# Weight loads on two DMA queues, and stores of gates and gated activations issued from ScalarE, in a hybrid decoder layer

## The chip, the cores and the metric

The kernel runs on one core of a Trainium2 chip. The metric is the device time of one execution in microseconds; the time before the change is the median of three runs. Engines are named as in the profile: PE is TensorE (PEld its weight loads), DVE is VectorE, ACT is ScalarE, POOL is GpSimd and SP is SyncE. "SPq" and "ACTq" stand for the instructions by which SP and ACT issue DMAs.

## What is computed

One decoder layer (DEPTH is 1) on 256 tokens of width 2048, all in float32:

```python
h = rmsnorm(x, g_mix)
proj = h @ w_in                        # 2048 x (3*2048 + 3*2048): q, k, v of 16 heads, three gates
gates = sigmoid(proj[..., 3 * MIX_WIDTH:])
o_a = stick_breaking_attention(...)    # 4 heads
o_b = moba_attention(...)              # 6 heads; here one causal block of 256 keys
o_c = dilated_attention(...)           # 6 heads, windows with dilations 1, 4, 16
merged = (gates[:, :, 0] * (flat(o_a) @ w_branch[:ea])
          + gates[:, :, 1] * (flat(o_b) @ w_branch[ea:eb])
          + gates[:, :, 2] * (flat(o_c) @ w_branch[eb:]))
x = x + merged @ w_out
h2 = rmsnorm(x, g_ffn)
gu = h2 @ w_gu                         # 2048 x 11264
x = x + (silu(gu[..., :D_FF]) * gu[..., D_FF:]) @ w_down    # 5632 x 2048
```

## The kernel before

**Products in two parts.** Each float32 operand is kept as a high part, rounded to float32r, and a low part, the difference. `product` (L162) makes one product of a 128x128 activation tile with a 128x512 weight tile from three matmuls (L164 high times high, L165 high times the weights' low part, L166 low times high). Weights come from HBM as tiles of 128 partitions x 2 x 512 (512 KB, two rows of tiles). `split` (L109) makes the parts: ACT casts to `w_hi`, DVE subtracts and writes `w_lo`. There are 5 buffers each for `w_hi` and `w_lo`.

**Column pairs.** q and k of the four groups of heads, the gates (but for two chunks) and all of w_gu are made two column chunks at a time by `project_pair` (L325). Of the 2048 rows, the chunks 0 and 1 (`WC`, 1024 rows) are multiplied by a scheme of seven products in place of eight, whose weights are partly sums of weight tiles; the other 1024 rows are multiplied plainly, by `rest` (L340). So a pair has two kinds of weight tiles:

- *Weights that sums are made of*, `g_raw`: four quarters, b11, b12, b21 and b22, of two tiles each, loaded by `quarter` (L312) through `load` (L282) into 6 buffers. DVE adds them into `u` (L321: b11 + b12) and changes them in place (`add_into`, L308 and L310). `begin_pair` (L315) loads b11, b12 and b21 of the next pair near the end of the current one (L376); b22 is loaded at L353.
- *Plain weights*, `w_raw`: eight tiles in a pair (four for each of the two column chunks), loaded by `rest` through `load` into 4 buffers, each read by one cast and one subtraction.

The results of a pair go to the PSUM accumulators X, Y (`ps` or `qs`) and Z, V (`z` and `v`, or, in the qk units, the other one of `ps` and `qs`). The seven products come as forms: 1 into X, 2 into Y, 5 into Z, then two plain tiles into V and Z (L354, L355), form 6, a plain tile, form 7, a plain tile, form 3, two plain tiles, form 4, two plain tiles. ACT copies X and Z to SBUF in between (`snapshot`, L303), since both are written again.

**The queues.** All weights are issued by SP, one after the other in the program's order: `fetch` (L105) pins each load to that order, and a load whose buffer isn't free holds all that follow. POOL issues the rest: the bias tables of a group's softmax (L657, two buffers, free when DVE has added the table, L588), the stores of the gates to the DRAM tile `gate_mem` (`keep_gate`, L673) and their loads (L777), x and x1 (L402, L810, L929), the stores of gated activations to `a_mem` (L865 and L879) and their loads `a_raw` (L900). ACT issues the DMA transposes of the gated activations (L852): a chunk made in pair c goes out during pair c + 1 (`turn_out`), comes back in pair c + 2, where ACT joins its halves (`turn_in`, L857) and, from chunk 3 on, it is stored to `a_mem`.

**Stages in time.** v, q, k and attention (to about 310 us), gates (310 to 555), w_branch (530 to 620), w_out (620 to 710), w_gu in 11 pairs (710 to 1170), w_down (from 1170 on; its loads don't go through `fetch`). The order of all instructions that aren't pinned is set by a scheduler when the program is built; it sees the changed queues and may place attention's steps elsewhere among the matmuls.

Of the kernel before, what the change touches and what calls it, by code (L numbers as in the profile page):

```python
# [18 lines left out]
P = 128  # L19
# [10 lines left out]
NB = 512  # L30
# [27 lines left out]
def hybrid_block(ctx: ExitStack, tc: tile.TileContext, x, w_in, w_branch, w_out, w_gu, w_down, rel_bias, xT, gains,  # L58
                 onehot, extra, out):
    nc = tc.nc  # L60
    x, out = x[0], out[0]
    w_in, w_branch, w_out, w_gu, w_down = (w[0] for w in (w_in, w_branch, w_out, w_gu, w_down))
# [36 lines left out]
    def banks():  # L99

        turn.reverse()
        return [acc.tile([P, NB], F32, name=turn[1]) for _ in range(2)]


    def fetch(dst, src):  # L105

        tc.keep_in_program_order(nc.sync.dma_start(dst, src))

    def split(hi, lo, src, pin=False):  # L109
        for op in nc.scalar.copy(hi, src), nc.vector.tensor_sub(lo, src, hi.bitcast(F32)):  # L110
            if pin:
                tc.keep_in_program_order(op)
# [169 lines left out]
    def load(w, k, col0, pl=None):  # L282

        raw = pl.tile([P, 2, NB], F32, name="g_raw", bufs=6 if pl is gx else 4) if pl else wpool.tile([P, 2, NB], F32, name="w_raw", bufs=4)
        (nc.sync.dma_start if w is w_down else fetch)(raw, w[k * P:(k + 2) * P, col0:col0 + NB].rearrange("(k p) n -> p k n", p=P))
        return raw

    def parts(src):
# [14 lines left out]
    def snapshot(ps):  # L303
        sb = half_kb()
        nc.scalar.copy(sb, ps)
        return sb
# [5 lines left out]
    def quarter(acts, w, kh, col0):  # L312
        return [load(w, 4 * c + 2 * kh, col0, gx) for c in acts.wc]

    def begin_pair(acts, w, colA, colB):  # L315

        b11, b12 = (quarter(acts, w, 0, col0) for col0 in (colA, colB))
        p11 = [parts(b) for b in b11]
        u = [gx.tile([P, 2, NB], F32, name="u") for _ in acts.wc]
        for a, b, d in zip(b11, b12, u):  # L320
            nc.vector.tensor_add(d, a, b)  # L321
        b21 = quarter(acts, w, 1, colA)
        return p11, b12, u, b21, [parts(b) for b in b21]

    def project_pair(acts, w, colA, colB, begun=None, nxt=None):  # L325

        cols = (colA, colB)
        X, Y = banks()  # L330
        Z, V = others()

        def form(ps, f, srcs, start, stop, split=False):
            for i, c in enumerate(acts.wc):
                wh, wl = srcs[i] if split else parts(srcs[i])
                for j in range(2):
                    product(ps, *acts.form(f, c, j), wh[:, j], wl[:, j], start and i + j == 0,
                            stop and i + j == len(acts.wc))

        def rest(n, k, p0, p1, start=False, stop=False):  # L340
            wh, wl = parts(load(w, k, cols[n]))
            for t, ps in ((1, p1), (0, p0)):
                for j in range(2):
                    product(ps, *acts.plain(t, k + j), wh[:, j], wl[:, j], bool(start and t == 1 and j == 0), stop and j == 1)

        ks = [k for c in range(KT // 4) if c not in acts.wc for k in (4 * c, 4 * c + 2)]
        p11, b12, u, b21, p21 = begun or begin_pair(acts, w, colA, colB)
        form(X, 1, p11, True, True, True)
        s1 = snapshot(X)
        form(Y, 2, p21, True, False, True)  # L350
        form(Z, 5, u, True, True)
        z5 = snapshot(Z)
        b22 = quarter(acts, w, 1, colB)  # L353
        rest(1, ks[0], Z, V, start=True)  # L354
        rest(1, ks[1], Z, V)  # L355
        add_into(u, b22)
        form(X, 6, u, False, True)
        x2 = snapshot(X)
        rest(1, ks[2], Z, V)
        add_into(b12, b22)  # L360
        form(X, 7, b12, False, True)
        x3 = snapshot(X)
        rest(1, ks[3], Z, V, stop=True)
        nc.vector.tensor_sub(z5, z5, x3)
        c22 = half_kb()
        nc.vector.tensor_add(c22, V, z5)
        form(Z, 3, b22, False, True)
        c12 = half_kb()
        nc.vector.tensor_sub(c12, Z, x2)
        for k in ks[:2]:  # L370
            rest(0, k, Y, X)
        add_into(u, b21)
        form(X, 4, u, False, False)
        for k in ks[2:]:
            rest(0, k, Y, X, stop=k == ks[-1])
        ahead = begin_pair(*nxt) if nxt else None  # L376
        c11 = half_kb()
        nc.vector.tensor_add(c11, Y, s1)
        return (c11, X, c12, c22), ahead
# [287 lines left out]
    gate_mem = dram.tile([3, 4, NT, P, NB], F32, name="gate_mem")  # L667

    def keep_gate(c, b, srcs):
        for t in range(NT):  # L670
            gt = half_kb()
            nc.scalar.activation(gt, srcs[t], AF.Sigmoid, scale=rstd[:, t:t + 1])
            nc.gpsimd.dma_start(gate_mem[b, c, t], gt)  # L673

    heads = {}

# [38 lines left out]
    def pair_of(kind, what):  # L715
        if kind == "qk":
            return hs, w_in, what * NB, NH * HD + what * NB
        if kind == "gates":
            return hs, w_in, gate_col(*what[0]), gate_col(*what[1])
# [13 lines left out]
    for (kind, what), after in zip(units, units[1:] + [(None, None)]):  # L733
        if kind == "gates" and what[0] == chunks[4]:
            finish_stages(slow_stages)
            pat.close()
            acc2 = ctx.enter_context(tc.tile_pool(name="acc2", bufs=1, space=PSUM))
            others = beside
            o = Columns(pool(ph1, "o", "left"), "o", NH)
            for i in range(NH // 4):  # L740
                at_split[split_count[0] + 22 * i + 12] = [lambda k=4 * i: split_o(k)]
        nxt = pair_of(*after)
        if kind in ("qk", "gates"):
            ps, ahead = project_pair(*pair_of(kind, what), ahead, nxt)
            if others is in_turn:
                turn.reverse()
        else:
            ps = project(h, 0, w_in, 0, KT, V0 + what * NB if kind == "v" else gate_col(*what),
                         *((ps0, FIRST) if (kind, what) == ("v", 0) else ()))
            ahead = begin_pair(*nxt) if nxt else None  # L750
        finish_stages(stages)
        if kind == "v":
            keep_v(what, ps)
        elif kind == "qk":
            keep_qk(what, *ps)
        elif kind == "gate":
            keep_gate(*what, ps)
        else:
            keep_gate(*what[0], ps[:2])
            keep_gate(*what[1], ps[2:])  # L760
# [11 lines left out]
    for c in range(4):  # L772
        ms = [half_kb() for _ in range(NT)]
        for b, (k0, nk) in enumerate(((0, H_A), (H_A, H_B), (H_A + H_B, H_C))):
            gt = [half_kb() for _ in range(NT)]
# [39 lines left out]
    for c in range(4):  # L815
        xc = load_x(c, nc.gpsimd.dma_start)
        ps = project(m, 0, w_out, 0, KT, c * NB)
        if c == 3:
            ahead = begin_pair(h2, w_gu, 0, D_FF)
        keep_x1(c, ps, xc)  # L820
    pm.close()
# [20 lines left out]
    a_mem = dram.tile([NF // 4, P, 4, S], F32, name="a_mem")  # L842
# [14 lines left out]
    def turn_in(c, t, keep):  # L857

        st = turning.tile([P, NB], F32, name="joined").rearrange("p (k q) -> p k q", k=4)
        tc.keep_in_program_order(nc.scalar.copy(st.bitcast(U16).rearrange("p k (q b) -> p b k q", b=2),  # L860
                                                keep[t].rearrange("p (b k) q -> p b k q", b=2)))
        if c < EARLY:
            at_split.setdefault(split_count[0] + IN_PARTS[t], []).append(lambda: a.put(c, t, st, True))
        else:
            nc.gpsimd.dma_start(a_mem[c, :, :, t * P:(t + 1) * P], st)  # L865

    def to_a_by_dma(c, srcs):

# [5 lines left out]
    def to_a(c, srcs):  # L874
        for t in range(NT):
            pt = transpose4(srcs[t])
            st = half_kb().rearrange("p (k q) -> p k q", k=4)
            nc.scalar.copy(st, pt)
            nc.gpsimd.dma_start(a_mem[c, :, :, t * P:(t + 1) * P], st)  # L879
            yield  # L880

    for c in ORDER[:EARLY]:
        a.place(pe, c)
    for c in range(D_FF // NB):
        nxt = (h2, w_gu, (c + 1) * NB, D_FF + (c + 1) * NB) if c + 1 < D_FF // NB else None
        (g0, g1_, u0, u1), ahead = project_pair(h2, w_gu, c * NB, D_FF + c * NB, ahead, nxt)
        sg = [half_kb() for _ in range(NT)]
        for t, (g, u) in enumerate(((g0, u0), (g1_, u1))):
            nc.scalar.activation(sg[t], g, AF.Silu, scale=rstd2[:, t:t + 1])
            nc.vector.scalar_tensor_tensor(sg[t], u, rstd2[:, t:t + 1], sg[t], op0=ALU.mult, op1=ALU.mult)  # L890
        if c < NF // 4 - 2:
            to_a_by_dma(c, sg)
        else:
            stages.append(to_a(c, sg))
# [153 lines left out]
```

## Time and profile before

| | |
|---|---|
| Median of 3 runs | 1428.85 us (1427.88 to 1429.82) |
| Profiled execution | 1427.54 us, span 1425.8 us |
| TensorE clock granted | 1.00 |
| HBM read | 293.17 MB |
| SP's queue (q1) | 277.38 MB, 58.0% of the 16 DMA engines' time |
| POOL's queue (q0) | 29.45 MB, 5.9% |
| ACT's queue (q10) | 5.80 MB, 2.8% |

How to read it: a busy time is the union of an engine's instructions. Matmuls are pipelined, so a busy PE may still lose time between the starts of its matmuls; its weight loads (PEld) don't overlap each other and show such gaps. An idle time names what ended it (`<-`). In the table of DMA issues the last number is the median time from issue to landing; in the view of a tile the three numbers of a group are the shortest, median and longest duration in ns. In the view of waits the numbers are microseconds in total, times, and the longest.

### The profile page before, as it was taken

What the parts mean: (1) busy time and instruction counts of PE and PEld (TensorE: products, weight loads), DVE (VectorE), ACT (ScalarE), POOL (GpSimd) and SP (SyncE); (2) the same over time, 40 slices, a digit from 0 to 9 for tenths busy, and PEclk for the clock granted to TensorE, in tenths of its full rate; (3) what the DMA queues carried; (4) which work ended last, traced back from release to release, by engine and by line L of the source; (5) the groups of instructions that cost most, each with busy time, mean ns of one, the idle gap of its engine ahead of it and who ended that gap; (6) DMA issues with size and microseconds to landing.
All of it is one profiled execution on the core that took longest, in us unless ns stands there. A gap on an engine that the chain in (4) does not pass through costs nothing. (4 is left out here: it accounts for less than half of the span.)

```text
span 1425.8 us, 17593 instructions
## 1 busy us (share of the span) xinstructions
PE 1411.4 (99%) x6297; PEld 1159.1 (81%) x6297; DVE 1190.0 (83%) x1265; ACT 909.5 (64%) x1160; POOL 65.1 (5%) x121
## 2 busy tenths in 40 slices
PE   8999999999999999999999999999999999999998
PEld 6888788888888888888888887778888888788887
DVE  7898797867799997876689999999999998886775
ACT  7767777767666665444456677676777776654453
POOL 1000000000000002100100000000000010100000
PEclk9999999999999999999999999999999999999999
DMA  9764547374656757866686667577977786776552
GB/s 331 277 221 135 205 134 247 108 250 162 222 177 236 256 195 276 297 224 213 220 299 221 216 190 233 187 219 244 268 223 218 250 237 228 251 238 235 191 172 94
DMA packets 174056, 313.76 MB, mean 220 GB/s; under 512 B 29800, under 2 KB 32384, under 8 KB 173968
## 3 DMA queue, kind: packets, MB, share of 16 engines
q1 hardware_dynamic: 144672, 277.38, 58.0%
q0 software_dynamic: 8992, 29.45, 5.9%
q10 hardware_dynamic: 20304, 5.80, 2.8%
q8 instruction: 49, 0.80, 0.2%
q14 instruction: 39, 0.32, 0.1%
HBM read 293.17 MB, written 14.70 MB: 216 GB/s over the span
## 5 line engine op out<-in xcount | busy, mean ns | idle before, releaser
L110 DVE TENSOR_TENSOR w_lo<-w_raw,w_hi 128x1024 fp32r<-128x1024 f32 x332 | 403.3, 1221 | 122.4 <-ACT w_hi L110 119.4
L110 ACT CAST w_hi<-w_raw 128x1024 fp32r<-128x1024 f32 x332 | 346.3, 1050 | 171.4 <-PE qs L166 53.4
L110 ACT CAST w_hi<-g_raw 128x1024 fp32r<-128x1024 f32 x184 | 190.8, 1052 | 111.2 <-PE ps L166 31.9
L110 ACT CAST w_hi<-u 128x1024 fp32r<-128x1024 f32 x138 | 145.0, 1053 | 155.5 <-DVE u L310 77.5
L110 DVE TENSOR_TENSOR w_lo<-g_raw,w_hi 128x1024 fp32r<-128x1024 f32 x184 | 219.1, 1220 | 30.0 <-ACT w_hi L110 29.0
L110 DVE TENSOR_TENSOR w_lo<-u,w_hi 128x1024 fp32r<-128x1024 f32 x138 | 164.3, 1220 | 21.4 <-ACT w_hi L110 20.8
L165 PE MATMUL ps<-w_lo,h_hi 128*128 128x512 f32 x352 | 137.9, 392 | 1.2 <-DVE w_lo L110 1.2
L166 PE MATMUL ps<-w_hi,h_lo 128*128 128x512 f32 x352 | 137.3, 390 | 0.0
L164 PE MATMUL ps<-w_hi,h_hi 128*128 128x512 f32 x352 | 131.9, 391 | 0.0
L165 PE MATMUL qs<-w_lo,h_hi 128*128 128x512 f32 x332 | 129.7, 391 | 0.0
L166 PE MATMUL qs<-w_hi,h_lo 128*128 128x512 f32 x332 | 129.2, 390 | 0.0
L164 PE MATMUL qs<-w_hi,h_hi 128*128 128x512 f32 x332 | 122.9, 391 | 0.0
L310 DVE TENSOR_TENSOR u<-u,g_raw 128x1024 f32<-128x1024 f32 x80 | 94.1, 1218 | 0.0
L165 PEld LDWEIGHTS ps<-w_lo,h_hi 128*128 128x128 f32 x352 | 66.1, 188 | 15.5 <-DVE w_lo L110 1.9
L166 PEld LDWEIGHTS ps<-w_hi,h_lo 128*128 128x128 f32 x352 | 66.1, 188 | 13.6
L164 PEld LDWEIGHTS ps<-w_hi,h_hi 128*128 128x128 f32 x352 | 65.9, 188 | 13.3
L166 PEld LDWEIGHTS qs<-w_hi,h_lo 128*128 128x128 f32 x332 | 62.3, 188 | 12.8
L165 PEld LDWEIGHTS qs<-w_lo,h_hi 128*128 128x128 f32 x332 | 62.3, 188 | 12.8
L164 PEld LDWEIGHTS qs<-w_hi,h_hi 128*128 128x128 f32 x332 | 62.3, 188 | 12.7
L321 DVE TENSOR_TENSOR u<-g_raw 128x1024 f32<-128x1024 f32 x40 | 48.7, 1219 | 20.9 <-DMA g_raw<-in_w_in 16.3
L165 PE MATMUL v<-w_lo,h_hi 128*128 128x512 f32 x120 | 48.0, 400 | 2.9 <-DVE w_lo L110 2.7
L310 DVE TENSOR_TENSOR g_raw<-g_raw 128x1024 f32<-128x1024 f32 x40 | 47.1, 1219 | 0.0
(386 smaller groups left out, 2940.8 us busy)
## 6 DMA issues: line engine op xcount, KB each, us to landing
w_raw<-in_w_in SPq DMA_DIRECT2D x116, 512.0 KB, 5.0
g_raw<-in_w_gu SPq DMA_DIRECT2D x88, 512.0 KB, 5.7
w_raw<-in_w_gu SPq DMA_DIRECT2D x88, 512.0 KB, 6.3
g_raw<-in_w_in SPq DMA_DIRECT2D x72, 512.0 KB, 5.4
w_raw<-in_w_down SPq DMA_DIRECT2D x64, 512.0 KB, 4.7
w_raw<-in_w_branch SPq DMA_DIRECT2D x32, 512.0 KB, 5.9
w_raw<-in_w_out SPq DMA_DIRECT2D x32, 512.0 KB, 4.7
g_raw<-in_w_down SPq DMA_DIRECT2D x24, 512.0 KB, 5.3
```

The lines of the kernel that those rows point to most:

```text
L110: for op in nc.scalar.copy(hi, src), nc.vector.tensor_sub(lo, src, hi.bitcast(F32)):
L164: nc.tensor.matmul(ps, ah, wh, start=start, stop=False, **how)
L165: nc.tensor.matmul(ps, ah, wl, start=False, stop=False, **how)
L166: nc.tensor.matmul(ps, al, wh, start=False, stop=stop, **how)
L310: tc.keep_in_program_order(nc.vector.tensor_add(d, d, a))
L321: nc.vector.tensor_add(d, a, b)
```

## The change

A second way to load is added, on POOL's queue, also pinned to the program's order. `load` uses it for `g_raw` tiles where the one-element list `own_queue` says so; plain tiles stay on SP's queue, and w_down's loads stay as they are. `own_queue` is switched to POOL with the first qk unit (so for its b22 and for all that is begun from then on), back to SP ahead of the `begin_pair` of w_gu's pair 0, and to POOL again from w_gu's pair 1 on. The pair that is begun inside pair 0 is loaded by SP.

The stores of the gates and those of the gated activations move from POOL's queue to ACT's.

```diff
+    def fetch_sums(dst, src):
+
+        tc.keep_in_program_order(nc.gpsimd.dma_start(dst, src))
+
+    own_queue = [fetch]
+
...
     def load(w, k, col0, pl=None):
...
-        (nc.sync.dma_start if w is w_down else fetch)(raw, w[k * P:(k + 2) * P, col0:col0 + NB].rearrange("(k p) n -> p k n", p=P))
+        (nc.sync.dma_start if w is w_down else own_queue[0] if pl else fetch)(raw, w[k * P:(k + 2) * P, col0:col0 + NB].rearrange("(k p) n -> p k n", p=P))
...
             nc.scalar.activation(gt, srcs[t], AF.Sigmoid, scale=rstd[:, t:t + 1])
-            nc.gpsimd.dma_start(gate_mem[b, c, t], gt)
+            nc.scalar.dma_start(gate_mem[b, c, t], gt)
...
         nxt = pair_of(*after)
+        if (kind, what) == ("qk", 0):
+            own_queue[0] = fetch_sums
...
         if c == 3:
+            own_queue[0] = fetch
             ahead = begin_pair(h2, w_gu, 0, D_FF)
...
         else:
-            nc.gpsimd.dma_start(a_mem[c, :, :, t * P:(t + 1) * P], st)
+            nc.scalar.dma_start(a_mem[c, :, :, t * P:(t + 1) * P], st)
...
             nc.scalar.copy(st, pt)
-            nc.gpsimd.dma_start(a_mem[c, :, :, t * P:(t + 1) * P], st)
+            nc.scalar.dma_start(a_mem[c, :, :, t * P:(t + 1) * P], st)
...
         nxt = (h2, w_gu, (c + 1) * NB, D_FF + (c + 1) * NB) if c + 1 < D_FF // NB else None
+        own_queue[0] = fetch_sums if c >= 1 else fetch
         (g0, g1_, u0, u1), ahead = project_pair(h2, w_gu, c * NB, D_FF + c * NB, ahead, nxt)
```

## The prediction

> **What bounds the kernel now.** I read the page's busy table first, then the profile cut into column pairs, then who waits for whom on TensorE's weight loads, and last the queues around one such wait.
>
> ```profile
> PE 1411.4 (99%) x6297; PEld 1159.1 (81%) x6297; DVE 1190.0 (83%) x1265; ACT 909.5 (64%) x1160; POOL 65.1 (5%) x121
> ```
>
> PE looks full: 1425.8 - 1411.4 leaves 14.4 us. But successive 128x512 matmuls start 0.23 us apart and each is shown as 0.39 us long, so short stalls hide inside "busy". The weight loads, 0.19 us each and one per matmul, show them. One pair is 180 such matmuls (14 sum tiles of 6, 8 plain tiles of 12). Here are four pairs of the w_gu stage, each cut from one pair's stall to the next:
>
> ```profile
> core 0: us, PE busy (x) PEld busy (x) DVE busy (x) ACT busy (x) POOL busy (x), PEclk, DMA share, GB/s
> 905.30:947.70 42.40, 41.54 (x180) 33.51 (x180) 39.90 (x39) 30.80 (x35) 0.00 (x0) 1.00 0.72 214
> 947.70:991.00 43.30, 43.01 (x187) 34.61 (x186) 39.35 (x38) 31.42 (x35) 2.15 (x3) 1.00 0.74 231
> 1032.60:1073.60 41.00, 41.00 (x181) 33.69 (x180) 38.20 (x37) 29.53 (x32) 1.44 (x2) 1.00 0.73 230
> 1114.90:1156.00 41.10, 41.10 (x187) 34.05 (x186) 38.81 (x38) 29.73 (x33) 1.43 (x2) 1.00 0.80 231
> ```
>
> The same work takes 41.0 us in one pair and 42.4 or more in another, at the full clock (1.00), with PE "busy" in both. The best pair sets PE's own price, about 41 us. DVE is busy 38 to 40 us of it: what DVE idles away while it waits for data, it can hardly make up. The lost time by its releaser, w_gu's pairs first, then the gates' pairs:
>
> ```profile
> PEld v L165 <- DVE w_lo L110: 5.1, 7, 1.1
> PEld ps L165 <- DVE w_lo L110: 1.7, 4, 0.5
> PEld qs L165 <- DVE w_lo L110: 0.8, 2, 0.5
> PEld v L164 <- ACT w_hi L110: 0.4, 1, 0.4
> PEld z L164 <- ACT sc L305: 0.2, 1, 0.2
> ```
>
> ```profile
> PEld v L165 <- DVE w_lo L110: 2.0, 4, 0.8
> PEld z L165 <- DVE w_lo L110: 0.8, 1, 0.8
> PEld qs L165 <- DVE w_lo L110: 0.3, 1, 0.3
> PEld ps L165 <- DVE w_lo L110: 0.3, 1, 0.3
> ```
>
> 8.2 us between 821 and 1120, 3.4 us between 380 and 530. Accumulator v is written first by the first plain tile of a pair (L354), so the plain tile is the late one. One such place, on SyncE's queue, ACT, DVE and the weight loads:
>
> ```profile
> 878.36 18.85 SPq L107 DMA_DIRECT2D g_raw<-in_w_gu  x8
> 897.31 17.59 SPq L107 DMA_DIRECT2D w_raw<-in_w_gu  x7
> ...
> 904.24 1.05 ACT L110 CAST w_hi<-w_raw 128x1024 fp32r<-128x1024 f32 x1 [2.65 <-DMA w_raw<-in_w_gu]
> ...
> 905.33 1.23 DVE L110 TENSOR_TENSOR w_lo<-w_raw,w_hi 128x1024 fp32r<-128x1024 f32 x1 [2.04 <-ACT w_hi L110]
> ...
> 905.35 0.19 PEld L164 LDWEIGHTS v<-w_hi,h_hi 128*128 128x128 f32 x1 [0.36 <-ACT w_hi L110]
> 906.61 0.19 PEld L165 LDWEIGHTS v<-w_lo,h_hi 128*128 128x128 f32 x1 [1.07 <-DVE w_lo L110]
> ```
>
> The chain is plain: eight g_raw loads hold SyncE's queue for 18.85 us, because each waits for its buffer; w_raw gets out only at 897.31; ACT sits 2.65 us for it, DVE 2.04 us, PE about 1.4 us, and the ps/qs waits come after it, while DVE catches up. It is the order of the queue and not the transfer rate, for the 16 DMA engines stand still meanwhile. In the DMA row of 1040 to 1080 us each digit is 1 us:
>
> ```profile
> DMA  8880007999999999980900388898999848898820
> ```
>
> **The change part by part.** *Sum weights to POOL's queue, plain ones alone on SyncE's.* From the first qk unit on, 66 g_raw loads of w_in and 74 of w_gu (the pairs 1 to 10, save the six that pair 0 starts for pair 1) leave SyncE's queue, and both streams then wait for their own buffers alone. A w_raw load goes out when one of its four buffers is read:
>
> ```profile
> 1047.19 1.22 DVE L110 TENSOR_TENSOR w_lo<-w_raw,w_hi 128x1024 fp32r<-128x1024 f32 x1
> ...
> 1063.15 2.08 SPq L107 DMA_DIRECT2D w_raw<-in_w_gu  x4
> ```
>
> DVE ends with a w_raw tile at 1048.4, and the load that can use its buffer leaves with three others at 1063.15: it would be 14.7 us earlier, against a lateness of 2.65. Removed: 8.2 + 3.4 = 11.6 us. The remaining waits (start, attention, w_branch, end) have other releasers, and I leave them.
>
> What a g_raw load costs on POOL has no row. The nearest:
>
> ```profile
> L107 SPq DMA_DIRECT2D g_raw<-in_w_gu x88: 367/368/1766, 707.7 to 1144.8; - x88
> L657 POOL DMA_DIRECT2D bias<-vec x6: 719/728/777, 18.5 to 259.8; - x6
> ...
> g_raw<-in_w_gu SPq DMA_DIRECT2D x88, 512.0 KB, 5.7
> a_raw<-a_mem POOLq DMA_DIRECT2D x8, 512.0 KB, 4.4
> sc<-in_x POOLq DMA_DIRECT2D x8, 256.0 KB, 6.7
> ```
>
> The bias load has the same 128x2 rows: 0.73 us of POOL to issue against 0.37 on SyncE; 8 in a pair are 5.8 us of an engine that is 5% busy. Landing is bounded by 4.4 us (a_raw, same bytes, longer rows) and 6.7 us (in_x). I take 6.5: SyncE's 5.7 for the same tile, plus 0.4 of issue, plus 0.4 for the w_raw loads now abreast. The load with least slack is the last pair before the next column pair (b21, freed by the sum of L372):
>
> ```profile
> 1051.32 1.50 SPq L107 DMA_DIRECT2D g_raw<-in_w_gu  x2
> ...
> 1059.30 1.06 ACT L110 CAST w_hi<-g_raw 128x1024 fp32r<-128x1024 f32 x1 [0.53 <-DVE u L321]
> 1061.79 1.06 ACT L110 CAST w_hi<-g_raw 128x1024 fp32r<-128x1024 f32 x1 [1.44 <-PE ps L166]
> ```
>
> Issue to first need is 8.0 us: 1.5 us to spare at 6.5, so nothing on the path. Without that cover each microsecond of lateness is one of PE's, since DVE has no reserve.
>
> The Trainium skill, "SBUF — State Buffer", section Who interferes with whom, speaks against this part: descriptor writing on GpSimd is shut out while DVE holds the port pair that the two share, in its two-port modes. The trace shows no such thing: with DVE busy 38 to 40 of 41 us, POOL's a_mem issues (row below) take 709 to 727 ns. If it bit, the b21 loads would be the ones to suffer, and the sum would be that of the slow rival.
>
> *What stands before g_raw in POOL's order.* Bias loads wait for DVE (third number the longest), and two a_raw loads wait for a store:
>
> ```profile
> POOL bias L657 <- DVE p L588: 202.7, 4, 125.4
> ...
> 1002.93 1.10 POOL L900 DMA_DIRECT2D a_raw<-a_mem  x2 [3.98 <-DMA a_mem<-joined]
> ```
>
> In the changed kernel's order the bias loads of a group come behind the g_raw loads of the unit in which their L588 runs; what is queued behind them (six loads begun for the next unit) is needed only at that unit's end, not at once. The a_raw pair sits between pair 6's last load and the first of pair 7:
>
> ```profile
> 1004.36 2.22 SPq L107 DMA_DIRECT2D g_raw<-in_w_gu  x4
> ...
> 1015.54 2.19 ACT L110 CAST w_hi<-g_raw 128x1024 fp32r<-128x1024 f32 x2
> ```
>
> It is out of POOL by 1004.0; SyncE sends the g_raw loads that follow at 1004.36 today, and the first is read 11 us later. Cost 0; without that cover, one wait of 4 us.
>
> *Stores on ACT.* 24 gate stores and 16 a_mem stores leave POOL and stand in ACT's order:
>
> ```profile
> L1013 ACTq DMA_DIRECT2D out<-sc x8: 338/339/363, 1300.8 to 1422.2; - x8
> L865 POOL DMA_DIRECT2D a_mem<-joined x12: 709/714/727, 948.8 to 1161.8; - x12
> ```
>
> Gate stores at ACT's own 0.34: 24 x 0.34 = 8.2 us. a_mem stores, with rows of 512 B, lie between 0.34 and 0.71, so 5.4 to 11.4; I take 0.5, near the SyncE price of 0.37 because ACT's queue, too, issues a whole tile in 0.34: 8 us. The 16 us lie where ACT waits anyway. The new order puts them just ahead of the snapshot of z and the casts of u, where ACT sits 2.00 us for DVE today:
>
> ```profile
> 909.92 2.19 ACT L110 CAST w_hi<-u 128x1024 fp32r<-128x1024 f32 x2 [2.00 <-DVE u L310]
> ```
>
> Four gate stores need 1.36 of those 2.00, an a_mem store 0.5. But what is queued behind them is that snapshot, and PE may not start Z without it (its 0.2 us row above). I charge 1 us over the whole kernel for it; bounds 0 and 16.
>
> *Sum.* Another 1.7 us for stalls that stay because DVE runs at 93 to 94% (an estimate of 0.1 us for each of 17 pairs, from the 0.1 by which the 41.1 us pair is over the 41.0 one). -11.6 + 1.0 + 1.7 = -8.9. The profiled execution took 1427.54 us (span 1425.8), so 1418.6; the median of the three runs is 1.3 above it, so **1419.9 us**.
>
> **The rivals.**
>
> *Half of it (DVE takes over).* The w_raw wait goes, but DVE at 38 to 40 us of 41 stays the pace, and the gain is that of the 7.1 us that v's L165 waits hold, less the same 2.7: 1424.4. For it: the waits are named DVE w_lo. Against: the 41.0 us pair, with the same DVE work.
>
> *No change.* The loads are late because the 16 engines are shared, and two queues only interleave what was in line. The pairs' DMA share is 0.72 to 0.80. Then all w_raw would land as late: 1428.9. Against it: the idle digits, and w_raw not being issued at all before 897.31. The Trainium skill, "DMA: Bandwidth & Descriptors", section Issuing engines are not separate DMA queues, says just this: several issuing engines save only the time of issuing. It does not speak of a queue that stands still for a buffer, which is what the rows show.
>
> *ACT is held.* The 16 us of stores are half uncovered: 1419.9 + 7 = 1426.9.
>
> *Slower: b21 late on POOL.* Place: the two loads freed by L372, in each of the 17 pairs started from POOL. If they take more than 8.0 us the casts wait, DVE idles, PE follows. At 9.5 us (in_x, half the bytes, takes 6.7; a second 256 KB transfer's worth on top) it is 1.5 us a pair, 17 x 1.5 = 25.5: 1419.9 + 25.5 = 1445. It decides from 8.0 + 8.9/17 = 8.5 us of landing on; below, the change still gains. For it: POOL's in_x needs longer for half the bytes than SyncE for the whole. Against: a_raw's 4.4.
>
> **How the numbers follow.** Forecast 0.60, its own range 1415.5 to 1423 (all 11.6 and a little of attention's waits; 6 us gained). Half 0.12; no change 0.10; ACT held 0.06; b21 late 0.12. The range goes to 1429, over every case but the last, and down to 1415: what is left out is 0.12 above and some 0.05 below. A change under 0.2% (2.9 us) cannot be told from none. Faster: 0.60 + 0.12 = 0.72. Same: 0.10 and two thirds of ACT held, 0.14. Slower: 0.12 and the rest, 0.14.
>
> **What would show it.** Right: SyncE's w_raw loads no longer come in fours after eight g_raw loads; ACT's waits for w_raw of w_gu (2.65 at 904) are gone; the w_gu pairs all take 41 to 41.3 us; v's L165 waits under 1 us in both windows. Wrong: casts of g_raw that wait for DMA by 1 us or more in each pair (b21 late), ACT idle before the snapshot of z behind its own stores, POOL issues of g_raw far over 0.73 us, or pairs of 42 us without any DMA wait.

## The result and the profile after

| | before | after |
|---|---|---|
| Median of 5 runs each | 1429.47 us (1427.88 to 1430.33) | 1470.53 us (1468.45 to 1475.59) |
| Ratio after/before, 95% interval | | 1.0294 [1.0273, 1.0316] |
| Span of the profiled execution | 1425.8 us | 1470.9 us |
| TensorE clock granted | 1.00 | 0.986 |

The kernel is 41.1 us slower; 8.9 us faster was forecast. In the new numbering L110 is L116 (`split`), L164 to L166 are L170 to L172 (`product`), L852 is L861 (transposes), and the `g_raw` loads of POOL have L111.

The busy table of the kernel after comes first.

```profile
PE 1422.8 (97%) x6297; PEld 1170.9 (80%) x6297; DVE 1193.9 (81%) x1265; ACT 910.0 (62%) x1160; POOL 141.8 (10%) x221
```

The work is the same: as many matmuls, DVE and ACT within 4 us of before. POOL's 100 more instructions take 77 us, close to what the prediction's prices give (140 loads more, 40 stores fewer). So the time went into waiting, and the profile cut into stretches says where. This is the kernel after, with the header line of that view.

```profile
core 0: us, PE busy (x) PEld busy (x) DVE busy (x) ACT busy (x) POOL busy (x), PEclk, DMA share, GB/s
400.00:450.00 50.00, 50.00 (x222) 41.41 (x221) 46.91 (x44) 35.52 (x41) 8.68 (x12) 1.00 0.72 229
850.00:900.00 50.00, 43.59 (x182) 35.52 (x181) 40.33 (x39) 30.54 (x34) 5.78 (x8) 0.93 0.84 178
950.00:1000.00 50.00, 42.67 (x180) 34.90 (x180) 38.81 (x37) 29.60 (x32) 6.56 (x10) 0.93 0.83 200
```

And the same stretches before.

```profile
400.00:450.00 50.00, 50.00 (x221) 40.98 (x221) 46.31 (x44) 35.95 (x41) 2.16 (x4) 1.00 0.63 215
850.00:900.00 50.00, 49.29 (x215) 39.80 (x214) 46.89 (x46) 34.57 (x40) 0.00 (x0) 1.00 0.66 210
950.00:1000.00 50.00, 49.49 (x216) 40.04 (x216) 46.95 (x44) 34.74 (x38) 2.14 (x3) 1.00 0.71 219
```

In the gates PE does slightly more in 50 us than before (41.41 us of weight loads against 40.98). In the two stretches of w_gu a stretch holds 180 to 182 matmuls where it held 215 or 216, the clock is 0.93, and the last two columns move against each other: the DMA engines are busier (0.83 or 0.84 against 0.66 to 0.71) and move less (178 and 200 GB/s against 210 and 219).

The waits of the kernel after: first PE's weight loads from 821 to 1190 us (w_gu), then ACT's longest of the same stretch, then PE's from 380 to 530 us (gates).

```profile
PEld qs L170 <- ACT w_hi L116: 20.9, 4, 6.0
PEld ps L170 <- ACT w_hi L116: 17.3, 3, 6.8
PEld qs L171 <- DVE w_lo L116: 0.8, 2, 0.5
```

```profile
ACT w_hi L116 <- DMA g_raw<-in_w_gu: 54.6, 13, 8.5
```

```profile
PEld z L171 <- DVE w_lo L116: 0.8, 1, 0.8
PEld v L171 <- DVE w_lo L116: 0.2, 1, 0.2
```

The waits of v, the plain tiles' accumulator, are nearly gone from both stages, as forecast: 2.0 us became 0.2 in the gates and 5.5 became 0 in w_gu. With the short waits of z, ps and qs that followed them, 3.4 us became 1.0 and 8.2 became 0.8. In w_gu, seven waits of 3.7 to 6.8 us at ps and qs (38.2 us) came in their place, behind casts of `g_raw` that waited for their DMA. One of them in order of time, kernel after:

```profile
883.58 16.99 SPq L107 DMA_DIRECT2D w_raw<-in_w_gu  x5
...
887.88 1.29 ACTq L861 DMA_TRANSPOSE turned<-sc  x1
890.74 0.72 POOL L111 DMA_DIRECT2D g_raw<-in_w_gu  x1 [3.29 <-DVE u L316]
892.16 0.72 POOL L111 DMA_DIRECT2D g_raw<-in_w_gu  x1 [0.70 <-DVE sc L372]
...
904.17 1.04 ACT L116 CAST w_hi<-g_raw 128x1024 fp32r<-128x1024 f32 x1 [6.20 <-DMA g_raw<-in_w_gu]
905.27 0.29 PEld L170 LDWEIGHTS qs<-w_hi,h_0hi 128*128 128x128 f32 x1 [4.44 <-ACT w_hi L116]
905.86 0.33 PEld L172 LDWEIGHTS ps<-w_hi,h_lo 128*128 128x128 f32 x1
906.29 0.33 PEld L170 LDWEIGHTS ps<-w_hi,h_hi 128*128 128x128 f32 x1
...
911.17 0.19 PEld L172 LDWEIGHTS qs<-w_hi,h_0lo 128*128 128x128 f32 x1
911.40 0.19 PEld L170 LDWEIGHTS qs<-w_hi,h_0hi 128*128 128x128 f32 x1
```

Read it upward from 905.27. PE waited for a cast, the cast for one of b21's two loads. That load left POOL at 890.74, on time, and needed 13 us. Three microseconds ahead of it ACT had issued a DMA transpose of gated activations.

The nine b21 quarters that POOL loads in w_gu behave alike. The casts would have needed the first of each two loads 7.2 to 7.8 us after its issue. PE lost what a landing took beyond 8.5 to 9.8 us: a landing of 8.8 us cost it nothing, one of 11.6 us cost 1.7 (at 809.9 us), and the seven of 12.8 to 15.8 us cost 3.7 to 6.8.

The last four lines of the view show a second cost. After the wait, weight loads start 0.43 us apart until about 911 and 0.23 apart from then on: PE runs at half its rate for some 5.5 us.

The DMA view of 888 to 904 us of the kernel after; each digit of the first line and each number of the second stands for 0.4 us:

```profile
DMA  9899995997999989999998995979999979999999
GB/s 318 307 374 353 256 246 184 374 307 266 371 363 331 165 109 170 161 127 129 155 191 127 161 140 150 153 150 235 192 228 245 214 235 291 405 420 389 420 399 338
```

From 893 to 899 the engines are as busy as ever and move 109 to 191 GB/s, about half or less of the 307 to 374 in the first four slices and the 389 to 420 in the five before the last. The table of queues (packets, MB, share of the 16 engines' time) tells whose packets these are, first for 893 to 899 us, then for 901.6 to 904:

```profile
q1 hardware_dynamic: 250, 0.47, 59.5%
q10 hardware_dynamic: 810, 0.21, 41.1%
q0 software_dynamic: 72, 0.27, 16.3%
```

```profile
q1 hardware_dynamic: 295, 0.56, 61.1%
q0 software_dynamic: 104, 0.39, 42.4%
```

Most of the transpose's quarter megabyte (q10) moves in the slow stretch. SP's loads (q1) hold as large a share of the engines there as behind it, and move 0.47 MB in 6.0 us where they then move 0.56 in 2.4. Over the whole kernel, issue to landing of `turned<-sc`, shortest, median and longest, before and then after:

```profile
DMA to landing us min/median/max: 2.7/5.8/11.6
```

```profile
DMA to landing us min/median/max: 7.2/14.9/21.1
```

The median landings in the kernel after:

```profile
w_raw<-in_w_gu SPq DMA_DIRECT2D x88, 512.0 KB, 6.7
g_raw<-in_w_gu POOLq DMA_DIRECT2D x74, 512.0 KB, 7.8
g_raw<-in_w_in POOLq DMA_DIRECT2D x66, 512.0 KB, 5.4
```

The same kind of load from the same queue lands in 5.4 us in the gates, where there are no transposes, and in 7.8 in w_gu.

**The account.** The waits of w_gu rose from 8.2 to 39.0 us, the gates' went down by 2.4. Half rate: between 821 and 1190 us 65 weight loads follow the one before by 0.40 to 0.45 us instead of 0.227, 7 to 12 after each of the seven waits; 65 x 0.2 = 13.0. Together 39.0 - 8.2 + 13.0 - 2.4 = 41.4 of the 45.1 us between the two spans. The other 3.7 us are not placed.

### The profile page after: what moved, and what is told of

It reads as the page before. It is cut to its first block, busy times and chain, and to the rows that moved or that the text cites. A ratio compares the mean times of both kernels' runs of the same rounds, so it can differ in the third digit from the quotient of the medians.

```text
span 1470.9 us, 17616 instructions
## 1 busy us (share of the span) xinstructions
PE 1422.8 (97%) x6297; PEld 1170.9 (80%) x6297; DVE 1193.9 (81%) x1265; ACT 910.0 (62%) x1160; POOL 141.8 (10%) x221
## 4 chain that ended last, share of the span: by engine, by line
PE 67%; DMA 12%; issue 9%; DVE 6%; ACT 3%; POOL 1%; SPq 0%; ACTq 0%; POOLq 0%; DVEq 0%
DMA g_raw<-in_w_gu 9%; PE qs L171 8%; PE qs L172 8%; PE ps L171 8%; PE qs L170 8%; PE ps L172 8%; PE ps L170 8%; DVE w_lo L116 3%; PE z L171 2%; PE z L170 2%; PE z L172 2%; ACT w_hi L116 2%; PE v L170 1%; PE v L171 1%; PE v L172 1%
## 5 line engine op out<-in xcount | busy, mean ns | idle before, releaser
L116 DVE TENSOR_TENSOR w_lo<-w_raw,w_hi 128x1024 fp32r<-128x1024 f32 x332 | 402.7, 1220 | 113.8 <-ACT w_hi L116 110.2
L116 ACT CAST w_hi<-w_raw 128x1024 fp32r<-128x1024 f32 x332 | 346.3, 1051 | 159.3 <-PE qs L172 50.6
L116 ACT CAST w_hi<-g_raw 128x1024 fp32r<-128x1024 f32 x184 | 191.3, 1051 | 155.0 <-DMA g_raw<-in_w_gu 58.5
L116 DVE TENSOR_TENSOR w_lo<-g_raw,w_hi 128x1024 fp32r<-128x1024 f32 x184 | 220.4, 1220 | 69.0 <-ACT w_hi L116 68.0
L116 ACT CAST w_hi<-u 128x1024 fp32r<-128x1024 f32 x138 | 145.1, 1053 | 164.3 <-DVE u L316 78.6
L116 DVE TENSOR_TENSOR w_lo<-u,w_hi 128x1024 fp32r<-128x1024 f32 x138 | 164.7, 1219 | 25.4 <-ACT w_hi L116 25.1
L171 PE MATMUL ps<-w_lo,h_hi 128*128 128x512 f32 x352 | 141.2, 401 | 1.7 <-DVE w_lo L116 1.7
L172 PE MATMUL ps<-w_hi,h_lo 128*128 128x512 f32 x352 | 140.6, 399 | 0.0
L170 PE MATMUL ps<-w_hi,h_hi 128*128 128x512 f32 x352 | 133.6, 397 | 0.0
L172 PE MATMUL qs<-w_hi,h_lo 128*128 128x512 f32 x332 | 131.3, 396 | 0.0
L170 PE MATMUL qs<-w_hi,h_hi 128*128 128x512 f32 x332 | 123.4, 394 | 0.0
L111 POOL DMA_DIRECT2D g_raw<-in_w_gu x74 | 53.5, 723 | 370.4 <-DVE w_lo L116 279.5
L111 POOL DMA_DIRECT2D g_raw<-in_w_in x66 | 47.7, 723 | 395.5 <-DVE w_lo L116 230.8
L172 PEld LDWEIGHTS ps<-w_hi,h_lo 128*128 128x128 f32 x352 | 68.1, 193 | 14.4
L170 PEld LDWEIGHTS ps<-w_hi,h_hi 128*128 128x128 f32 x352 | 66.9, 191 | 14.0 <-ACT w_hi L116 0.2
L172 PEld LDWEIGHTS qs<-w_hi,h_lo 128*128 128x128 f32 x332 | 63.6, 192 | 13.4
L170 PEld LDWEIGHTS qs<-w_hi,h_hi 128*128 128x128 f32 x332 | 63.0, 190 | 12.9
```

The lines of the kernel that those rows point to most:

```text
L111: tc.keep_in_program_order(nc.gpsimd.dma_start(dst, src))
L170: nc.tensor.matmul(ps, ah, wh, start=start, stop=False, **how)
L171: nc.tensor.matmul(ps, ah, wl, start=False, stop=False, **how)
L172: nc.tensor.matmul(ps, al, wh, start=False, stop=stop, **how)
```

## The experiments

Theory **T1**: a DMA transpose on ACT's queue and ordinary weight loads slow each other when they are in flight together, and b21, which has the least slack, is then late. SP's queue of before, standing still for a buffer, left the transposes nearly alone with the engines. **T1a** says any load queue does it, **T1b** that it takes POOL's and SP's together. Rival **R1**: loads issued from POOL are late in themselves, or ACT is held by its stores.

Each ratio is to runs of the kernel before that were taken with it.

| Kernel | us | ratio to before, 95% |
|---|---|---|
| e1: after, w_gu's sums back on SP | 1424.79 | 0.9962 [0.9949, 0.9976] |
| e2: after, gates' sums back on SP | 1483.70 | single run |
| e3: after, TensorE transposes | 1426.24 | 0.9976 [0.9966, 0.9985] |
| e4: before, TensorE transposes | 1429.36 | 1.0000 [0.9987, 1.0013] |
| e5: after, transposes at the pair's end | 1428.08 | 0.9990 [0.9978, 1.0002] |
| e6: before, transposes at the pair's end | 1462.75 | 1.0234 [1.0219, 1.0248] |
| e7: after, w_gu's plain weights on POOL, sums on SP | 1424.51 | single run |
| e8: before, two plain tiles ahead of b21 | 1419.70 | 0.9932 [0.9919, 0.9945] |
| e10: before, stores from ACT | 1429.58 | 1.0003 [0.9994, 1.0013] |
| e11: e8 and the gates' sums on POOL | 1441.11 | 1.0084 [1.0071, 1.0097] |
| e12: e11 and stores from ACT | 1419.35 | 0.9927 [0.9913, 0.9940] |

### Which stage: e1 and e2

e1 is the changed kernel without the switch of w_gu; e2 is the changed kernel without the switch of the qk units and gates.

```diff
-        own_queue[0] = fetch_sums if c >= 1 else fetch
```

> The changed kernel, but the sum weights of w_gu stay on SyncE's queue (those of w_in on GpSimd's; gate and a_mem stores from ScalarE's). Theory T1: ordinary loads and ScalarE's DMA transposes slow each other when they are in flight together, and SyncE's standing queue had left the transposes room; there are no transposes before 800 us, so this kernel keeps the 3 us that the gates' pairs gained and loses nothing: 1424 to 1427. Rival R1: loads issued by GpSimd are late in themselves, or ScalarE's stores hold it: slower than before, 1432 or more.

```diff
-        if (kind, what) == ("qk", 0):
-            own_queue[0] = fetch_sums
```

> The changed kernel, but the sum weights of w_in stay on SyncE's queue (those of w_gu on GpSimd's). T1: all the loss is in w_gu, 1470 to 1476, transposes land in about 15 us. R1: about half of the loss, 1450.

e1 gives 0.4% and e2 loses more than the whole change, so the loss sits in w_gu, and the rest of the change (the qk units, the gates and the stores) is a gain by itself. In e1 the transposes land in 6.0 us (median), with the stores on ACT and POOL loading in the gates; that speaks against R1. e2 came out above the 1470 to 1476 expected. Its span is 11.0 us over that of after: the gates' waits are back at 4.0 us (3.0 more), w_gu's from 821 to 1200 us are 41.7 (2.7 more), and between 380 and 1210 us there are 85 half-rate starts instead of 66 (3.8 more). The remaining 1.5 us are not placed.

### Without DMA transposes: e3 and e4

Both put all chunks through the path that the kernel already has for its last ones, TensorE transposes (`to_a`), e3 on the changed kernel and e4 on the one before.

```diff
-            nc.scalar.dma_start(a_mem[c, :, :, t * P:(t + 1) * P], st)
+            if c < EARLY:
+                a.put(c, t, st)
+            else:
+                nc.scalar.dma_start(a_mem[c, :, :, t * P:(t + 1) * P], st)
...
-        if c < NF // 4 - 2:
-            to_a_by_dma(c, sg)
-        else:
-            stages.append(to_a(c, sg))
+        stages.append(to_a(c, sg))
```

> The changed kernel with all chunks of gated activations turned by TensorE (as the last two are), no DMA transpose at all. T1: without transposes the two queues gain what was forecast: 5 to 11 us under e4, all landings in w_gu under 9 us. R1 (loads from GpSimd are late in themselves beside SyncE's): 30 us or more over e4.

> The kernel before with all chunks of gated activations turned by TensorE, no DMA transpose. Both theories: 72 more transposes on TensorE at 0.12 to 0.27 us, so 1436 to 1448; it is the base for e3.

With POOL still loading `g_raw` in w_gu, the whole loss is gone. POOL's loads land in 5.7 us, close to the 5.4 of the gates, so POOL is not slow in itself, and R1's first half falls:

```profile
g_raw<-in_w_gu POOLq DMA_DIRECT2D x74, 512.0 KB, 5.7
```

e4 missed its expectation, and it bears on the prediction. SP's queue there still sends eight `g_raw` loads ahead of the plain ones and stands in them for 19 us, pair after pair. In the timeline of e4:

```profile
1002.57 18.87 SPq L107 DMA_DIRECT2D g_raw<-in_w_gu  x8
1021.49 22.47 SPq L107 DMA_DIRECT2D w_raw<-in_w_gu  x8
```

And yet no weight load waits for anything between 821 and 1190 us: the view of waits is empty there. Two windows of 100 us show PE busy throughout at the full clock:

```profile
850.00:950.00 100.00, 100.00 (x455) 83.03 (x454) 94.50 (x90) 64.24 (x76) 2.23 (x4) 1.00 0.62 211
950.00:1050.00 100.00, 100.00 (x451) 82.86 (x450) 92.40 (x86) 64.95 (x73) 4.70 (x7) 1.00 0.67 224
```

So the 8.2 us of waits in w_gu do not come from the queue's order alone. That the time does not fall fits the price of the transposes on TensorE. In e4, 821 to 1190 us:

```profile
L186 PE MATMUL tr<-ident,sc 128*128 128x128 f32 x72 | 10.3, 272 | 0.0
```

Before had 8 of these in the same stretch (1.2 us): 9.1 us more of PE, about what the removed waits give. That is some 1.1 us more in each of eight pairs, which also gives late loads more time. How much of the removed waits is owed to that, and how much to the absent DMA transposes, these two kernels can't tell apart: the median landing of w_raw fell from 6.3 to 5.9 us, and ACT's longest wait for it from 2.7 to 0.8. With w_gu free of waits from 821 us on in both, e3 is ahead of e4 by the gates alone: 3.1 us by the medians, short of the 5 to 11 expected, with 1.0 against 3.8 us of waits from 380 to 530.

### Transposes at another place: e5 and e6

`to_a_by_dma` issues its two transposes behind the 14th and 18th split of a pair, and b21's loads leave between the two. Both kernels issue them at the end of the pair instead; e5 on the changed kernel, e6 on the one before. The halves are joined three splits later than they were.

```diff
-        for t, (out_at, in_at) in enumerate(((14, 3), (18, 7))):
+        for t, (out_at, in_at) in enumerate(((22, 6), (24, 10))):
```

> The changed kernel with the two DMA transposes of a pair issued at the pair's end (after the casts 22 and 24 instead of 14 and 18) and read back three casts later, where the changed kernel's DMA engines stood idle for 5 us. T1 (transposes and ordinary loads slow each other when in flight together): transposes land in 4 to 8 us, loads of w_gu in under 9, and the kernel takes 1418 to 1428. If the place makes no difference (loads from GpSimd's queue and transposes disturb each other for another reason): 1460 or more.

> The kernel before with the same move of the transposes: there, six loads of SyncE's queue go out at the pair's end. T1a (any load beside a transpose is enough): transposes land in 10 us or more, loads late, 1440 to 1470. T1b (it takes loads from GpSimd's queue beside those of SyncE's): transposes land in 6 to 9 us and the time stays within 6 us of before.

e5 keeps the queues of the change, and moving 18 transposes takes 42 us off. Landings in w_gu of e5, and those of its transposes:

```profile
g_raw<-in_w_gu POOLq DMA_DIRECT2D x74, 512.0 KB, 6.0
turned<-sc ACTq DMA_TRANSPOSE x18, 5.1
```

The forecast gain does not appear, though: 5.8 us of short waits of qs, ps and v for `w_lo` remain from 821 to 1190. e6 is the mirror image. One load queue, as before, and the move costs 33 us, because SP's plain tiles now meet the transposes. PE's waits in w_gu of e6:

```profile
PEld v L164 <- ACT w_hi L110: 16.1, 9, 4.2
PEld v L165 <- DVE w_lo L110: 8.9, 13, 1.1
```

From 821 to 1190 us all of PE's waits are 35.8 us here and were 8.2 before. The time is what T1a expected, though the transposes land in 8.4 us (median), under the 10 it named. Two load queues are not needed for the loss, against T1b: a load with little slack beside a transpose is enough.

### The other way round: e7

After, but in w_gu POOL's queue carries the plain weights and SP's the sums'. Both queues are in flight as in the changed kernel, and the transposes are where they were.

```diff
-        (nc.sync.dma_start if w is w_down else own_queue[0] if pl else fetch)(raw, ...)
+        (nc.sync.dma_start if w is w_down else own_queue[0] if bool(pl) == (w is w_in) else fetch)(raw, ...)
```

> The changed kernel with the queues of w_gu exchanged: the sums' weights on SyncE's queue, the plain ones on GpSimd's. T1 and T1b: as slow as the changed kernel, 1455 to 1485, transposes in 10 us or more. If it is the lateness of the sums' weights alone that costs: under 1440.

1424.5 us in a single run: both T1 and T1b had expected 1455 and more. The other clause of the expectation, that the lateness of the sums' weights alone costs, is the one that came. In e7:

```profile
turned<-sc ACTq DMA_TRANSPOSE x18, 10.7
g_raw<-in_w_gu SPq DMA_DIRECT2D x88, 512.0 KB, 7.0
w_raw<-in_w_gu POOLq DMA_DIRECT2D x80, 512.0 KB, 5.9
```

```profile
ACT w_hi L116 <- DMA g_raw<-in_w_gu: 22.7, 9, 5.3
```

The transposes are slower than before (10.7 against 5.8) and it costs 5.4 us of PE's waits in all. ACT waits 22.7 us for b21's kind instead of 54.6, and 5.3 at most instead of 8.5; the first two microseconds or so of each never reach PE (at 905 us in the kernel after 6.20 at ACT became 4.44 at PE). What costs is thus how late b21 is, not that transposes are slow or that two queues are in flight. Why POOL's `g_raw` and SP's `w_raw` hold the transposes up more than the reverse is open.

### The order alone, on one queue: e8

The kernel before, all weights on SP, but the first two plain tiles of the next pair are loaded ahead of b21's quarter instead of behind all eight `g_raw` loads. Buffers, bytes and engines are the same.

```diff
     def begin_pair(acts, w, colA, colB):
...
+        first = [load(w, k, colB) for k in (8, 10)]
...
-        rest(1, ks[0], Z, V, start=True)
-        rest(1, ks[1], Z, V)
+        rest(1, ks[0], Z, V, start=True, raw=first[0])
+        rest(1, ks[1], Z, V, raw=first[1])
```

> The kernel before with all weights on SyncE's queue, but the first two plain tiles of the next pair issued after its b12 and ahead of its b21 (so the late loads go out some 13 us earlier without a second queue, and two more loads are in flight beside the transposes). T1b: the forecast gain without the loss, 1418 to 1423, transposes in 6 to 9 us. T1a: transposes in 10 us or more and no gain or slower, 1430 or more.

1419.70 us, 0.7% under before. PE's waits from 821 to 1190 in e8:

```profile
PEld qs L164 <- ACT w_hi L110: 0.7, 1, 0.7
PEld ps L164 <- ACT w_hi L110: 0.7, 1, 0.7
```

The gain that the prediction put on the second queue is there, and it takes no second queue. The transposes land in 8.2 us (median) and nothing is late enough to matter. This is the outcome that T1b expected, and T1a missed it. With e6 and e7 it narrows the theory: neither one queue nor two decides, and a transpose beside loads costs only where it makes the load of least slack late.

### The stores, and the best of both: e10, e11, e12

e10 is the kernel before with the stores of gates and gated activations moved to ACT, and nothing else.

```diff
-            nc.gpsimd.dma_start(gate_mem[b, c, t], gt)
+            nc.scalar.dma_start(gate_mem[b, c, t], gt)
```

> The kernel before with one part of the change alone: the 24 gate stores and the 16 stores of gated activations are issued by ACT; all weights stay on SP's queue, in the old order. If the stores are as cheap as the prediction had it (1 us in all) and are not what slows the changed kernel: 1428 to 1432 us, transposes landing in about 6 us as before. If ACT held by its own stores has a part in the loss (rival R1): 1435 us or more, with waits of the snapshots of z or of the casts of u behind ACT in the w_gu pairs.

1.0003 [0.9994, 1.0013]: nothing, within 2 us. That ends R1's second half. e11 puts e8's order and the change's part in the qk units and gates together (w_gu's weights on SP, the stores left on POOL).

> Two gains put together: the two plain tiles loaded ahead of b21's quarter (all pairs), and the sums' weights of the qk units and gates on POOL's queue as in the change, but w_gu's weights all on SP. The stores stay on POOL. If the gain of POOL's queue in the gates is the removed wait for the plain tiles (3.4 us in 380 to 530), the reorder has already taken it there, and the two don't add: 1418 to 1422 us. If POOL's queue brings something of its own in the gates (both streams waiting for their own buffers alone): 1414 to 1417 us. Under T1 the w_gu stage is the same as with the reorder alone, since no transpose meets a load from POOL.

Neither expectation held: 1441.11 us, 21 slower than e8. The two largest groups of e11's waits from 320 to 560 us, the gates, of 23.2 us in all where e8 has 1.0:

```profile
PEld ps L170 <- ACT w_hi L116: 9.9, 2, 5.0
PEld qs L171 <- DVE w_lo L116: 4.1, 4, 1.1
```

And POOL's and DVE's order of time at the first:

```profile
432.62 2.33 POOL L680 DMA_DIRECT2D gate_mem<-sc  x4 [15.00 <-ACT sc L679]
434.95 1.45 POOL L111 DMA_DIRECT2D g_raw<-in_w_in  x2
...
443.46 1.22 DVE L316 TENSOR_TENSOR u<-u,g_raw 128x1024 f32<-128x1024 f32 x1 [6.67 <-DMA g_raw<-in_w_in]
```

POOL stands for 15 us at the first of four gate stores until ACT has made its sigmoid, and b22's two loads, which come behind them in POOL's order, leave at 434.95. DVE's sum for form 6 waits 6.67 us for them, PE 5.0. e12 moves the stores to ACT and changes nothing else.

> The run before with one edit more: the gate stores and the stores of gated activations are issued by ACT, as in the change. In that run four gate stores sat on POOL ahead of b22's two loads and waited 15.0 us for ACT's sigmoid (to 432.62), and the loads left at 434.95; TensorE then lost 5 us at 440 and at 536 and some 2 us at each of two more places. If that is the whole of the difference to the reorder alone, this kernel takes 1416 to 1422 us, and no wait in 320 to 560 is over 1 us. If POOL's queue and the reordered plain tiles harm each other in another way (for instance by being in flight together), it stays above 1432 us.

b22's loads then leave at 423.54, 11 us earlier:

```profile
423.54 1.57 POOL L111 DMA_DIRECT2D g_raw<-in_w_in  x2 [8.71 <-DVE w_lo L116]
```

e12 takes 1419.35 us. The third part of the change is free by itself (e10) and worth 22 us as soon as POOL loads weights (e11 to e12). e8 and e12 are equal within their intervals and beat both kernels; of the two, e8 needs seven lines and no second queue.

## Why the prediction was wrong

**The step that failed is the landing of b21**: "I take 6.5: SyncE's 5.7 for the same tile, plus 0.4 of issue, plus 0.4 for the w_raw loads now abreast". It was worked out from other loads, and left out the DMA transposes that ACT issues just there. The trace of before had them: 18, landing in 5.8 us at the median, 2.7 at best and 11.6 at worst. Those of 2.7 us had at most one load beside them, the one of 11.6 had eight. In the changed kernel the first b21 load of each quarter in w_gu took 8.8 to 15.8 us beside a transpose, and 12.8 or more in the seven quarters that cost most. The slack of 8.0 us was about right (7.2 to 7.8 to the cast). The sum also had no price for the clock, which added 13.0 us to the waits. e3 and e5 show that the transposes make the difference, since either takes the loss away with all of POOL's loads in place.

**"It is the order of the queue and not the transfer rate, for the 16 DMA engines stand still meanwhile"** was half true. The order alone mends it (e8), but in w_gu so does moving the transposes to TensorE (e4). And the pause was counted as pure loss. Idle DMA engines were the room in which a transpose landed in 2.7 us; in the changed kernel, where each had loads of both queues beside it, the quickest took 7.2.

**Point by point.** The w_raw waits: right, 8.2 and 3.4 us became 0.8 and 1.0. The gates: right, and measured by e1 with the qk units and the stores: its ratio of 0.9962 is a gain of 5.4 us (3.4 to 7.3), against 3.4 forecast for the gates. POOL's issue of a `g_raw` load: 0.72 us, forecast 0.73; DVE's load on the shared port did not show. The rule of the Trainium skill that was weighed there ("SBUF — State Buffer", section Who interferes with whom) speaks of DVE's two-port modes, and the same section says that tensor_tensor, DVE's operation in all the rows shown here, has none. So the 709 to 727 ns that were held against the rule hardly test it. POOL's order ahead of `g_raw`: right at cost 0 for the kernel as changed. What the prediction did not see is how much of that rests on the gate stores having left (e11). ACT's stores: 1 us forecast, 0.4 measured (e10: 0.03% of 1429, interval -0.9 to 1.9), which can't be told from nothing. The 1.7 us for stalls that stay can't be told apart from the rest.

**The rivals.** The slow one named the place, the load and the point from which it decides, 8.5 us, and its chain came: b21 late, casts that wait, PE behind them. Its reason for the lateness, a slow landing of POOL's own loads, did not (5.7 us in e3), and its price was far too low (1445): it took 1.5 us in each of 17 pairs. The gates, with no transposes, lost nothing, and w_gu lost 3.7 to 6.8 us in each of seven pairs and the clock on top. "No change", with transfers that only interleave, was nearer to the cause than the chance of 0.10 says, but it made no transfer slower than before, and that is what happened.

## What to carry to other kernels

A queue that stands still for a buffer is a loss to what is queued behind it and a gain to what runs beside it. Before freeing it, list every transfer that is in flight in that pause, DMA transposes above all, and price the load of least slack with those beside it. And try the order first: e8 reached the forecast time by moving two loads ahead of two others on one queue. An engine that is to issue loads with deadlines must not have stores ahead of them that wait for another engine's result (e11 against e12).

## What was not expected of the hardware

**Transposes and loads together.** With a transpose in flight beside loads of two queues, 16 busy engines moved 109 to 191 GB/s from 893 to 899 us, against 389 to 420 some microseconds later. The 256 KB of a transpose took 7.2 to 21.1 us to land in that kernel. The Trainium skill, "Advanced Engine Details and Errata", section X-Bar Transpose (TRN2), has transposes as fast as ordinary DMAs. The trace of before comes near that for a transpose that has the engines to itself: from 893.4 to 894.1 us one moved 273 to 307 GB/s, and it landed in 2.7 us. Beside loads it did not hold in the kernel after: 256 KB took 14.9 us at the median, against 6.7 and 7.8 for the loads' 512 KB, and the loads slowed too. Why the engines, busy as they were, moved so little is not shown.

**Half rate after a wait.** Each of the seven waits of 3.7 us and more in w_gu was followed by 7 to 12 matmuls starting 0.43 us apart, and the granted clock of these 50 us was 0.93; the wait of 1.7 us that ended at 809.9 us was followed by none. It turned 39.0 us of waits into 52. The Trainium skill, "TensorE: Matmul & The Clock Gate", section What's actually happening, has the clock halved after an idle window of about 3.4 us, and full again after about as long at work. Its section Wait — 56ns, not 53.3ns? gives 426.7 ns between starts for 512 columns at half clock. The trace agrees with all three: 0.43 us between starts, waits of 3.7 us that set it off and one of 1.7 that did not, and 7 to 12 starts, which are 3.0 to 5.2 us. The other kernels narrow it down: one wait of 3.6 us set it off (e7), one of 3.5 did not (e2), and two of 2.7 and 1.5 us close together did (e2). So the price of a wait has a step. By an estimate from the 13.0 us of half rate after seven waits, seven waits of 4 us would cost some 41 us here, and not 28.
